# Conditioning products on four 32-column parts, plain, and layer 0's shift and scale made in quarters of the columns

## The chip, the cores and the metric

One core of one Trainium2 chip runs the whole program. The metric is the device time of one execution in microseconds (us), the median of several runs. TensorE (PE, with its weight loads as PEld), VectorE (DVE), ScalarE (ACT), GpSimd (POOL) and SyncE (SP, which here issues the transfers of weights) each work through a queue of their own in order.

## What is computed

The reference runs two transformer blocks over 256 tokens of width 1024. The change lies in the first block, which has two layers and also carries 256 context tokens. Each layer first makes a modulation of 3072 columns from a conditioning vector, once for the latent tokens and once for the context tokens:

```python
def layer(x, cx, c_silu, cctx_silu, norm_w, ada_w, ada_b, w_in, w_out, ...):
    mod = c_silu @ ada_w + ada_b
    mod_c = cctx_silu @ ada_w + ada_b
    shift, scale, gate = jnp.split(mod, 3, axis=-1)
    hx = rmsnorm(x, norm_w) * (1 + scale[:, None, :]) + shift[:, None, :]
    hc = rmsnorm(cx, norm_w) * (1 + scale_c) + shift_c
    px = split_cols(hx @ w_in)          # queries, keys, values of three mixers, and a gate of 1536
    ...                                  # three kinds of attention
    ux = jnp.concatenate([ya, yb, yc_], axis=-1) * jax.nn.silu(px[9])
    x = x + gate[:, None, :] * (ux @ w_out)
```

So the product with `ada_w` (1024 x 3072, two layers, 25 MB in all) has only two rows, and `hx`, from which everything else follows, can't be made before shift and scale of its columns are there. The rest (the second block: feed-forward, two sparse attentions, feed-forward, twice) isn't touched.

## The kernel before

All weights come in tiles of 128 partitions x 1024 elements (512 KB), in the order of `weight_plan`. SP loads tile after tile into staging buffers `ws` (18 of their own for the start, then four in turn, `LOOK`), ACT copies a tile into a rounded high part `wh` (L283) and DVE makes the low part `wl` (L284), three buffers of each, and PE multiplies a matrix product as three rounded products: high x high, high x low, low x high (`three`, L423 to L425). As soon as DVE has split a tile, its staging buffer is free for the next transfer.

A conditioning tile holds two chunks of 128 rows by 512 columns, and there are 48 of them. The first 16 (layer 0's shift and scale, in two halves of the columns) are multiplied as they are, in full precision, out of the staging buffers (L748): the conditioning is a 32-column weight operand `cst1`, and the tile's two chunks go to columns 0 to 31 and 32 to 63 of the array, so to two 32-row strips of one accumulator `psm`. A plain product stands as two records in the trace. The other 32 (layer 1's, and layer 0's gate) are split like all weights and multiplied in rounded form, four products to a tile, against an 8-column operand `cst4` that holds the high and low parts of the conditioning (L751, L753). These are the fills: they are spread over the products that make gate columns 4 to 11 of layer 0, four tiles within each (`gate` in `layer1`), eight tiles to an accumulator.

When an accumulator is done, `ada_close` copies it (ACT, L764), adds its rows up and turns them with four small products (L767), and DVE adds the bias and forms 1 + scale (L778, L783).

`start` orders the beginning: `norm_rows` makes the normalised rows `xn` and `cn`, then for each half of the columns `cond` multiplies eight tiles and closes, `half` turns the rows on PE (`turn_pair`, L812), applies scale and shift on ACT (`ht`, L821) and splits the result on DVE into `hT` (L824, L825); `gate` multiplies the first four gate columns with what is there of `hT`. All later products need the whole of `hT`. A scheduler places the instructions on each engine's queue, by priorities in the order written and by what is ready; PE does them in that order.

Attention runs between the weight products. Its last step multiplies probabilities and values on two 64-column parts of the array (L609), 4 to 20 products to an accumulator.

## Time and profile before

| | us |
|---|---|
| median of 3 runs | 1919.62 (1919.45 to 1920.26) |
| the profiled execution's own time | 1919.23 |
| its span, first to last instruction | 1917.4 |
| PE busy in it | 1876.4 |
| DVE busy | 1263.4 |
| ACT busy | 1094.2 |

The span is the profiled execution without what lies around it, 1.8 us. PE's busy time is that of pipelined products whose ends are modelled: two products that follow each other closely overlap in it, so what one costs is read from start to start and not from its duration.

### The profile page before, as it was taken

How to read it: one execution, taken by the hardware profiler on the slowest of the kernel's cores; microseconds unless marked ns; L12 is line 12 of the kernel's file. 1: busy time of each engine (PE TensorE's matmuls, PEld its weight loads, DVE VectorE, ACT ScalarE, POOL GpSimd, SP SyncE). 2: the span in 40 equal slices, each digit the busy share in tenths (PEclk: the TensorE clock that was granted, in tenths of full speed). 3: DMA queues.
4: the chain of work that ended last, by engine and by line, in shares of the span. 5: the costliest groups of instructions: out<-in, count | busy, mean ns of one | idle time of the engine just before them, and what ended most of it. 6: DMA issues, size and time to landing. Idle time of an engine off the chain costs nothing.

```text
span 1917.4 us, 27602 instructions
## 1 busy us (share of the span) xinstructions
PE 1876.4 (98%) x10332; PEld 1549.6 (81%) x10332; DVE 1263.4 (66%) x2476; ACT 1094.2 (57%) x1971; POOL 4.9 (0%) x14
## 2 busy tenths in 40 slices
PE   7999999999999999999999999999999999999998
PEld 3777788877988977888888878888888888888886
DVE  3476856788586787555688565555555689575555
ACT  3467757785567675444477655445444558655443
POOL 0000000000000000000000000000000000000000
PEclk9999999999999999999999999999999999999999
DMA  7334344136432238554434665554555333555551
GB/s 310 109 121 133 120 99 133 67 122 210 134 98 86 69 110 291 188 182 148 123 104 130 229 209 187 188 186 176 191 186 183 115 102 115 199 184 178 187 185 68
DMA packets 85670, 295.16 MB, mean 154 GB/s; under 512 B 10144, under 2 KB 10656, under 8 KB 85536
## 3 DMA queue, kind: packets, MB, share of 16 engines
q1 hardware_dynamic: 80304, 282.34, 45.2%
q10 hardware_dynamic: 5136, 11.04, 1.8%
q8 instruction: 81, 1.33, 0.3%
q14 instruction: 53, 0.43, 0.1%
q0 software_dynamic: 96, 0.01, 0.1%
HBM read 292.30 MB, written 1.06 MB: 153 GB/s over the span
## 4 chain that ended last, share of the span: by engine, by line
PE 90%; DVE 6%; ACT 2%; DMA 1%; issue 1%; SPq 0%; ACTq 0%; DVEq 0%
PE acc L423 24%; PE acc L425 24%; PE acc L424 23%; PE pso L609 4%; PE pst L577 4%; PE pss L511 2%; PE pss L512 2%; DVE wl L284 2%; PE psr L714 1%; PE psx L1195 1%; PE psr L720 1%; PE psm L1277 1%; DMA ws<-in_wall 1%; PE acc L751 1%; PE acc L753 1%
## 5 line engine op out<-in xcount | busy, mean ns | idle before, releaser
L284 DVE TENSOR_TENSOR wl<-ws,wh 128x1024 fp32r<-128x1024 f32 (+3 forms) x530 | 628.0, 1187 | 455.9 <-ACT wh L283 454.7
L283 ACT CAST wh<-ws 128x1024 fp32r<-128x1024 f32 (+3 forms) x530 | 541.4, 1024 | 531.3 <-PE acc L425 476.9
L423 PE MATMUL acc<-wh,xt 128*128 128x512 f32 (+3 forms) x1120 | 416.2, 375 | 1.6 <-ACT wh L283 1.6
L424 PE MATMUL acc<-wl,xt 128*128 128x512 f32 (+3 forms) x1120 | 415.2, 371 | 1.4 <-DVE wl L284 1.4
L425 PE MATMUL acc<-wh,xt 128*128 128x512 f32 (+3 forms) x1120 | 414.8, 372 | 0.0
L424 PEld LDWEIGHTS acc<-wl,xt 128*128 128x128 f32 x1120 | 211.0, 188 | 34.1 <-DVE wl L284 2.9
L423 PEld LDWEIGHTS acc<-wh,xt 128*128 128x128 f32 x1120 | 210.5, 188 | 34.1 <-ACT wh L283 2.3
L425 PEld LDWEIGHTS acc<-wh,xt 128*128 128x128 f32 x1120 | 210.6, 188 | 32.7 <-issue 0.7
L423 PE MATMUL acc<-wh,hT 128*128 128x384 f32 (+2 forms) x480 | 159.5, 333 | 0.0
L424 PE MATMUL acc<-wl,hT 128*128 128x384 f32 (+2 forms) x480 | 158.6, 330 | 0.0
L425 PE MATMUL acc<-wh,hT 128*128 128x384 f32 (+2 forms) x480 | 157.9, 329 | 0.0
L547 ACT ACTIVATE p<-pss,nm 128x512 f32<-128x512 f32 (+2 forms) x240 | 127.7, 541 | 27.7 <-DVE nm L530 12.0
L423 PE MATMUL acc<-wh,hffn 128*128 128x512 f32 x352 | 137.8, 391 | 0.0
L425 PE MATMUL acc<-wh,hffn 128*128 128x512 f32 x352 | 137.1, 390 | 0.0
L424 PE MATMUL acc<-wl,hffn 128*128 128x512 f32 x352 | 137.0, 389 | 0.0
L577 PE MATMUL pst<-consts,p 128*128 128x128 f32 x624 | 101.4, 277 | 0.8 <-ACT pt L593 0.7
L423 PEld LDWEIGHTS acc<-wh,hT 128*128 128x128 f32 x480 | 90.6, 189 | 6.4 <-issue 0.4
L424 PEld LDWEIGHTS acc<-wl,hT 128*128 128x128 f32 x480 | 90.7, 189 | 5.5 <-issue 0.4
L425 PEld LDWEIGHTS acc<-wh,hT 128*128 128x128 f32 x480 | 90.6, 189 | 4.5 <-issue 0.4
L577 PEld LDWEIGHTS pst<-consts,p 128*128 128x128 f32 x624 | 73.0, 140 | 24.1 <-ACT pt L593 4.9
L569 ACT ACTIVATE p<-p,rinv 128x256 f32<-128x256 f32 (+2 forms) x152 | 81.3, 577 | 11.6 <-DVE rinv L563 8.5
L425 PEld LDWEIGHTS acc<-wh,hffn 128*128 128x128 f32 x352 | 66.1, 188 | 13.9
(302 smaller groups left out, 2825.8 us busy)
## 6 DMA issues: line engine op xcount, KB each, us to landing
ws<-in_wall SPq DMA_DIRECT2D x476, 512.0 KB, 3.4
ws<-in_wall SPq DMA_DIRECT2D x64, 384.0 KB, 3.2
bias<-in_bias ACTq DMA_DIRECT2D x8, 512.0 KB, 3.9
cx<-in_ctx SPq DMA_DIRECT2D x2, 1024.0 KB, 6.7
ws<-in_wall SPq DMA_DIRECT2D x4, 420.0 KB, 3.1
gt<-gates ACTq DMA_DIRECT2D x3, 512.0 KB, 4.6
x<-in_x SPq DMA_DIRECT2D x1, 1024.0 KB, 6.8
out<-y SPq DMA_DIRECT2D x2, 512.0 KB, 2.6
```

The costliest lines, as they stand in the source:

```text
L283: self.nc.scalar.copy(h[:, :n], s[:, :n])
L284: self.nc.vector.tensor_tensor(lo[:, :n], s[:, :n], h[:, :n].bitcast(F32), op=ALU.subtract)
L423: mm(out, ah, bh, start=start, stop=False)
L424: mm(out, ah, bl, start=False, stop=False)
L425: mm(out, al, bh, start=False, stop=stop)
L511: nc.tensor.matmul(S[:, o:o + w], q, kh, start=True, stop=False)
L512: nc.tensor.matmul(S[:, o:o + w], q, kl, start=False, stop=True)
L547: nc.scalar.activation(p[:, o:o + w], S[:, o:o + w], AF.Exp, bias=nm[:, i:i + 1], accum_out=sm[:, i:i + 1])
L569: nc.scalar.activation(p[:, o:o + w], p[:, o:o + w], AF.Copy, scale=r[:, i:i + 1])
L577: nc.tensor.transpose(t[:, i * P:(i + 1) * P], sl["P"][:, o:o + P], self.ident)
L609: nc.tensor.matmul(O[HD * i:HD * i + HD, c:c + w], v, p, start=y < 2, stop=y >= len(todo) - 2)
L714: nc.tensor.transpose(p[:, 2 * a + g, :], ks[:, t, a, g, :], self.ident_r)
```

## The change

It does five things. First, every conditioning tile is now used plain, out of its staging buffer, and two tiles are taken together: `ada_pair` multiplies their four chunks on four 32-column parts of the array (columns 0, 32, 64 and 96) into the four strips of one accumulator, the later tile's chunks first. The rounded form, `cst4` and its preparation are gone. Second, layer 0's shift and scale are made in four quarters: a quarter has 256 columns of scale and 256 of shift, four tiles, and is followed in the plan by one tile of two row chunks of `w_in` for gate columns 0 to 3 (`quarter_tiles`); after a quarter is closed, two column chunks of `hT` follow, and 24 gate products on them. Third, a fill takes its two pairs after row chunks 1 and 6 of a gate column; the plan puts the second pair behind the first tile of the next item, and `w_hold` fetches that tile ahead. Fourth, a staging buffer that holds a plain tile becomes free only when its products are done: `_pump` stops at such a tile, and is called again behind each pair. Fifth, `in_a_row` writes each group of products on parts (the four of a pair, and attention's of one accumulator) so that the scheduler puts nothing between them.

```diff
-START_TILES = 18
-START_PLAIN = [*range(8), *range(9, 17)]
+START_TILES = 5 * QUARTERS
...
+def quarter_tiles(i):
+    w = r_(1024 + 256 * i, 256) + r_(256 * i, 256)
+    return split_tiles("ada_w", 0, KD, w) + [("w_in", 0, r_(2 * i, 2), r_(3072, P * GATE_START))]
...
+            plan += t[:1] + late + t[1:]
+            n = it[2] if gate else 0
+            plan += fill[:n // 2]
+            late, fill = fill[n // 2:n], fill[n:]
...
-        if self.si in START_PLAIN:
+        if name == "ada_w":
             self.split[self.si] = (s, s)
+            self.plain.add(self.si)
...
+    def _pump(self):
         while self.di < min(max(self.si, START_TILES) + self.LOOK + self.more * (self.di < self.more_end), len(self.plan)):
+            if self.di - self.LOOK >= START_TILES and self.di - self.LOOK in self.plain:
+                break
             self._dma()
...
+    def in_a_row(self, todo):
+        def mm(out, a, b, start, stop):
+            return self.nc.tensor.matmul(out, a, b, start=start, stop=stop)
+        first = mm(*todo[0])
+        with self.tc.issue_after(getattr(first, "ins", first)), self.tc.high_priority():
+            for x in todo[1:]:
+                mm(*x)
...
+    def ada_pair(self, g):
+        b = g["n"] // 2
+        todo = []
+        for j in range(2):
+            ks, _, w, _ = self.w_next("ada_w", *g["blocks"][b])
+            todo += [(kk, w[:, i, :]) for i, kk in enumerate(ks)]
+        self.in_a_row([(g["bank"][32 * i:32 * i + 32, :], self.cst1[:, kk, 28 - 4 * b:60 - 4 * b], w,
+                        g["n"] == 0, g["n"] == g["last"]) for i, (kk, w) in enumerate(todo[::-1])])
+        self.plain -= {self.wi - 2, self.wi - 1}
+        self._pump()
         g["n"] += 1
...
+        quarter(0)
+        self.gate_acc = [self.acc() for _ in range(GATE_START)]
+        for i in range(QUARTERS):
+            ks, _, wh, wl = self.w_next("w_in", 0, 3072)
             for a, kk in enumerate(ks):
+                for j in range(GATE_START):
+                    self.three(self.gate_acc[j], ...
+                if a == 0 and i + 1 < QUARTERS:
+                    quarter(i + 1)
...
-                    if k * n // KD < (k + 1) * n // KD:
+                    if n and k in (1, 6):
+                        if k == 6:
+                            self.w_hold()
                         self.fill = self.fill or self.ada_open(self.fills.pop(0), "a")
-                        self.ada_tile(self.fill)
+                        self.ada_pair(self.fill)
```

Three places show what moves. On PE at the very start, the queue before has the first half's eight tiles (`ws`, two products each), its close (`psr`) and the first turned rows (`psx`):

```order
L748 MATMUL psm_221<-ws_121,cst_100 32x512 x2
L748 MATMUL psm_221<-ws_123,cst_100 32x512 x2
L748 MATMUL psm_221<-ws_125,cst_100 32x512 x2
L748 MATMUL psm_221<-ws_127,cst_100 32x512 x2
L748 MATMUL psm_221<-ws_129,cst_100 32x512 x2
L748 MATMUL psm_221<-ws_131,cst_100 32x512 x2
L748 MATMUL psm_221<-ws_133,cst_100 32x512 x2
L748 MATMUL psm_221<-ws_135,cst_100 32x512 x2
L767 MATMUL psr_252<-consts,mod_250 128x4 x4
L812 MATMUL psx_263<-consts,xn_0_159 128x128 x4
L812 MATMUL psx_273<-consts,xn_1_160 128x128 x4
```

and now:

```order
L446 MATMUL psm_215<-ws_113,cst_94 32x512 x2
L446 MATMUL psm_215<-ws_111,cst_94 32x512 x2
L446 MATMUL psm_215<-ws_117,cst_94 32x512 x2
L446 MATMUL psm_215<-ws_115,cst_94 32x512 x2
L792 MATMUL psr_238<-consts,mod_236 128x2 x4
L859 MATMUL psx_246<-consts,xn_0_153 128x128 x4
L859 MATMUL psx_256<-consts,xn_1_154 128x128 x4
L455 MATMUL acc_266<-hT_0_100,wh_228 128x512
```

The close and the first turned rows stand behind four tiles instead of eight, and gate products follow them at once. On PE in the first gate column with fills (gate column 4; `wh`, `wl` and `hT` make the gate product, `cst` the fill), before:

```order
L423 MATMUL acc_687<-hT_0_110,wh_615 128x512
L424 MATMUL acc_687<-hT_1_111,wh_615 128x512
L425 MATMUL acc_687<-hT_0_110,wl_616 128x512
L751 MATMUL acc_694<-wh_645,cst_96 8x512
L753 MATMUL acc_694<-wl_646,cst_96 8x512
L751 MATMUL acc_694<-wh_645,cst_96 8x512
L753 MATMUL acc_694<-wl_646,cst_96 8x512
L423 MATMUL acc_687<-hT_0_110,wh_615 128x512
```

and now the second pair of the same gate column:

```order
L457 MATMUL acc_680<-hT_0_100,wl_621 128x512
L446 MATMUL acc_687<-ws_696,cst_94 32x512 x2
L446 MATMUL acc_687<-ws_624,cst_94 32x512 x2
L455 MATMUL acc_680<-hT_0_100,wh_620 128x512
L456 MATMUL acc_680<-hT_1_101,wh_620 128x512
```

Four rounded products to a tile become four plain ones to two tiles, and they read `ws` itself. Fifteen gate products lie between the first pair and this one. On SP the transfers of the tiles around it, with what each waits for, before:

```order
L257 DMA ws_559<-in_wall 128x1024 [waits DMAHW7_49,DMAHW3_49,DVE_49]
L257 DMA ws_589<-in_wall 128x1024 [waits DMAHW0_49,DVE_49]
L257 DMA ws_619<-in_wall 128x1024 [waits DMAHW5_49,DMAHW1_49,DVE_49]
L257 DMA ws_649<-in_wall 128x1024 [waits DMAHW6_49,DMAHW2_49,DVE_49]
L257 DMA ws_685<-in_wall 128x1024 [waits DMAHW3_49,DVE_49]
```

and now:

```order
L264 DMA ws_624<-in_wall 128x1024 [waits DMAHW7_49,DMAHW5_49,DVE_49]
L264 DMA ws_696<-in_wall 128x1024 [waits DMAHW4_49,DVE_49]
L264 DMA ws_698<-in_wall 128x1024 [waits DMAHW3_49,PE_49]
L264 DMA ws_700<-in_wall 128x1024 [waits DMAHW2_49,DMAHW0_49,PE_49]
L264 DMA ws_824<-in_wall 128x768 [waits DMAHW6_49,DMAHW1_49,PE_49]
L264 DMA ws_826<-in_wall 128x1024 [waits DMAHW5_49,PE_49]
```

Where every transfer waited for DVE's split of an earlier tile, those that follow a plain tile in its buffer now wait for PE. From layer 0's output product on, the queues of all engines stand as before.

## Rows read from the trace of the kernel before

**Rows 1.** The page: span, busy time and instructions by engine, and the chain that ended last.

```profile
span 1917.4 us, 27602 instructions
PE 1876.4 (98%) x10332; PEld 1549.6 (81%) x10332; DVE 1263.4 (66%) x2476; ACT 1094.2 (57%) x1971; POOL 4.9 (0%) x14
...
PE 90%; DVE 6%; ACT 2%; DMA 1%; issue 1%; SPq 0%; ACTq 0%; DVEq 0%
```

**Rows 2.** Groups of PE instructions, 65 to 340 us: busy us, mean ns, idle before.

```profile
L425 PE MATMUL acc<-hT,wl 128*128 128x512 f32 x65 | 26.1, 402 | 1.2 <-DVE wl L284 1.2
...
L753 PE MATMUL acc<-wl,cst 128*8 128x512 f32 x64 | 25.4, 398 | 0.1
L751 PE MATMUL acc<-wh,cst 128*8 128x512 f32 x64 | 25.4, 397 | 0.0
```

**Rows 3.** Timeline of PE, one fill tile: start us, us, engine, line, operation.

```profile
88.17 0.40 PE L751 MATMUL acc<-wh,cst 128*8 128x512 f32 x1
...
89.09 0.40 PE L423 MATMUL acc<-hT,wh 128*128 128x512 f32 x1
```

**Rows 4.** Timeline of TensorE in the start, its weight loads (PEld) at one place.

```profile
12.10 7.37 PE L748 MATMUL psm<-ws,cst 128*32 128x512 f32 x24 [12.10 <-DMA ws<-in_wall]
...
19.70 0.14 PEld L748 LDWEIGHTS psm<-ws,cst 128*32 128x32 f32 x4 [1.14 <-DMA ws<-in_wall]
19.70 1.05 PE L748 MATMUL psm<-ws,cst 128*32 128x512 f32 x4 [0.23 <-DMA ws<-in_wall]
...
20.97 1.05 PE L748 MATMUL psm<-ws,cst 128*32 128x512 f32 x4 [0.22 <-DMA ws<-in_wall]
22.76 1.05 PE L767 MATMUL psr<-consts,mod 64*128 64x4 f32 x8 [0.73 <-ACT mod L764]
23.74 0.65 PE L812 MATMUL psx<-consts,xn 128*128 128x128 f32 x4
...
36.75 0.39 PE L425 MATMUL acc<-hT,wl 128*128 128x512 f32 x1
37.07 6.20 PE L748 MATMUL psm<-ws,cst 128*32 128x512 f32 x26
43.19 0.50 PE L423 MATMUL acc<-hT,wh 128*128 128x512 f32 x1
...
54.03 1.20 PE L423 MATMUL acc<-hT,wh 128*128 128x512 f32 x4 [0.17 <-DVE hT L824]
...
65.05 0.39 PE L423 MATMUL acc<-wh,hT 128*128 128x512 f32 x1
```

**Rows 5.** Timeline of PE: plain products on one 32-column part, 128 columns each.

```profile
948.92 6.27 PE L1277 MATMUL psm<-w,mv 128*32 128x128 f32 x56 [0.23 <-issue]
```

**Rows 6.** Timelines of ACT and DVE in the start.

```profile
24.48 1.02 ACT L821 ACTIVATE ht<-psx,mod 128x256 f32<-128x256 f32 x2 [1.78 <-DVE mod L778]
...
51.22 1.92 ACT L821 ACTIVATE ht<-psx,mod 128x256 f32<-128x256 f32 x4
...
17.02 1.41 DVE L804 TENSOR_SCALAR xn<-cx,rstd 128x1024 f32<-128x1024 f32 x2
```

**Rows 7.** Busy time by stretch: us, engines (instructions), PEclk granted, DMA share, GB/s.

```profile
26.00:28.00 2.00, 2.00 (x4) 0.18 (x2) 2.00 (x3) 2.00 (x5) 0.00 (x0) 0.50 1.04 414
28.00:30.00 2.00, 2.00 (x7) 0.90 (x6) 1.88 (x4) 1.00 (x3) 0.00 (x0) 0.65 1.02 406
...
100.00:120.00 20.00, 19.51 (x113) 14.89 (x112) 17.75 (x38) 9.58 (x14) 0.00 (x0) 1.00 0.59 201
```

**Rows 8.** The page: splitting of weight tiles, and transfers (KB, us to landing).

```profile
L284 DVE TENSOR_TENSOR wl<-ws,wh 128x1024 fp32r<-128x1024 f32 (+3 forms) x530 | 628.0, 1187 | 455.9 <-ACT wh L283 454.7
L283 ACT CAST wh<-ws 128x1024 fp32r<-128x1024 f32 (+3 forms) x530 | 541.4, 1024 | 531.3 <-PE acc L425 476.9
...
ws<-in_wall SPq DMA_DIRECT2D x476, 512.0 KB, 3.4
```

**Rows 9.** Timeline of PE: attention's products on two parts, broken once.

```profile
226.80 0.65 PE L609 MATMUL pso<-pt,VG 128*64 128x256 f32 x4
227.39 0.55 PE L577 MATMUL pst<-consts,p 128*128 128x128 f32 x3
227.86 3.24 PE L609 MATMUL pso<-pt,VG 128*64 128x256 f32 x28
```

More of the change, by code (lines that the diff above doesn't have):

```diff
@@ L69 @@
 ]
-def gate_half_tiles(h):
-    return [("w_in", 0, r_(4 * h, 4), r_(3072 + 256 * i, 256)) for i in range(GATE_HALF // 2)]
+def quarter_tiles(i):
+    w = r_(1024 + 256 * i, 256) + r_(256 * i, 256)
+    return split_tiles("ada_w", 0, KD, w) + [("w_in", 0, r_(2 * i, 2), r_(3072, P * GATE_START))]
 WOUT_KS = [[0, 1], [4, 2], [3, 5], [8, 9], [6, 10], [11, 7]]
@@ L107, in weight_plan @@
     plan = []
-    a = [[t for l, c0 in g for t in ada_tiles(l, [c0])] for g in ADA_HALF + [sum(ADA_FILL, [])]]
-    g = [gate_half_tiles(h) for h in range(2)]
-    plan += a[0] + g[0][:1] + a[1] + g[0][1:] + g[1]
-    fill = a[2]
+    for i in range(QUARTERS):
+        plan += quarter_tiles(i)
+    fill = [t for l, c0 in sum(ADA_FILL, []) for t in ada_tiles(l, [c0])]
     for l in range(DEPTH):
+        late = []
         for it in ITEMS[l]:
-            if it[0] == "g":
-                plan += split_tiles("w_in", l, KD, r_(3072 + 128 * it[1], 128)) + fill[:it[2]]
-                fill = fill[it[2]:]
-            else:
-                plan += split_tiles("w_in", l, KD, bundle_cols(*it))
+            gate = it[0] == "g"
+            t = split_tiles("w_in", l, KD, r_(3072 + P * it[1], P) if gate else bundle_cols(*it))
+            plan += t[:1] + late + t[1:]
+            n = it[2] if gate else 0
+            plan += fill[:n // 2]
+            late, fill = fill[n // 2:n], fill[n:]
         for stream in range(2 if l == 0 else 1):
@@ L171, in const_table @@
     put("ident", np.eye(P))
+    e = np.arange(P)[:, None] % 32
+    put("sel2", (2 * (e // 4) + e % 4 == np.arange(16)[None, :]) & (e % 4 < 2))
     nf = HD // 4
@@ L194, in const_table @@
     put("hsel", (np.arange(64)[:, None] // 16 == np.arange(4)[None, :]).astype(np.float32))
[L195 to L196 removed]
     return [np.concatenate(x, 1).astype(np.float32) for x in parts], where
+FIRST = P + 16
 COLS = {}
@@ L235, in __init__ @@
         self.ratio = 1.0
+        self.plain = set()
+        self.held = None
         self.flags = set()
@@ L607, in f_v @@
                 todo += [(i, c + pair[2], P, v, p) for i, c, v, p in pair[1].get("extra", [])]
-            for y, (i, c, w, v, p) in enumerate(todo):
-                nc.tensor.matmul(O[HD * i:HD * i + HD, c:c + w], v, p, start=y < 2, stop=y >= len(todo) - 2)
+            self.in_a_row([(O[HD * i:HD * i + HD, c:c + w], v, p, y < 2, y >= len(todo) - 2)
+                           for y, (i, c, w, v, p) in enumerate(todo)])
             for pair in pairs:
@@ L735, in ada_open @@
     def ada_open(self, blocks, kind):
[L736 to L755 removed]
+        return dict(blocks=blocks, bank=self.acc() if kind == "a" else self.ps(kind), n=0, last=len(blocks) * 2 - 1)
@@ new lines, in ada_cols @@
+    def ada_cols(self, g):
+        nb = len(g["blocks"])
+        self.uid += 1
+        m = self.junk.tile([P, 512], F32, tag="junk", name=f"mod{self.uid}")
+        self.nc.scalar.copy(m, g["bank"])
+        p = self.ps("r")
+        for j in range(4):
+            self.nc.tensor.matmul(p[:, 16 * j:16 * j + 2 * nb], m[:, j * P:(j + 1) * P], self.cst("sel2")[:, :2 * nb],
+                                  start=True, stop=True)
+        return p[:, :64].rearrange("p (j b s) -> p s b j", b=8, s=2)
@@ new lines, in ada_quarter @@
+    def ada_quarter(self, i):
+        nc = self.nc
+        g = self.ada_open([(0, 1024 + 256 * i)], "m")
+        for _ in range(2):
+            self.ada_pair(g)
+        pv = self.ada_cols(g)[:, :, 0, :]
+        for a, j in ((8, 0), (0, 2)):
+            o = a + 2 * i
+            nc.vector.tensor_tensor(self.mod[0][:, :, o:o + 2], pv[:, :, j:j + 2],
+                                    self.col("ada_b", o, 2)[:, None, :].to_broadcast([P, 2, 2]), op=ALU.add)
+        o = 8 + 2 * i
+        nc.vector.scalar_tensor_tensor(self.mod[0][:, :, o:o + 2], self.mod[0][:, :, o:o + 2], 1.0,
+                                       self.col("norm_w", 2 * i, 2)[:, None, :].to_broadcast([P, 2, 2]),
+                                       op0=ALU.add, op1=ALU.mult)
@@ L760, in ada_close @@
         nb = len(g["blocks"])
-        self.uid += 1
-        m = self.junk.tile([P, 512], F32, tag="junk", name=f"mod{self.uid}")
-        rows = g.get("rows", 4 * nb)
-        nc.scalar.copy(m[:rows, :], g["bank"][:rows, :])
-        p = self.ps("r")
-        for j in range(4):
-            nc.tensor.matmul(p[:, 16 * j:16 * j + 2 * nb], m[:rows, j * P:(j + 1) * P],
-                             self.cst("sel2")[:rows, :2 * nb], start=True, stop=True)
-        pv = p[:, :64].rearrange("p (j b s) -> p s b j", b=8, s=2)
+        pv = self.ada_cols(g)
         b = 0
```

79 lines of the change are left out of this document (22 added, 57 removed).

## The prediction

> **What bounds the kernel now.** I read the page first: PE is busy 98% of the span and carries 90% of the chain that ended last [rows 1], so I looked for places where PE itself does less, or waits less. The groups by line between 65 and 340 us came next [rows 2]: the rounded fills are 128 products there, and PE hardly waits for their parts; the one visible wait in that stretch is 1.2 us for DVE's `wl`. A timeline of one fill tile gives its price [rows 3]: from its first product at 88.17 to the next gate product at 89.09 is 0.92 us, four products at 0.23 us, in a stream without a hole. So a fill tile removed from PE's queue there is 0.92 us off the end, as long as nothing else becomes the bound. The start is different: its timeline [rows 4] shows PE waiting for weights until 12.10, for single tiles until 20.97, and then working nearly without a stop until the first product that needs the whole of `hT`, at 65.05. That moment is the start's measure.
>
> **Part by part. Fills on four parts.** Before: 32 tiles x 0.92 = 29.4 us on PE. Now: 16 groups of four plain products. The rows show two parts at work, never four. On one part, 56 records of 128 columns take 6.27 us, 0.112 us each, so 0.448 us for 512 columns and 0.90 us for a product of two records [rows 5]. On two parts, 26 records take the 6.12 us from 37.07 to 43.19, 0.235 us each [rows 4]: twice the rate, the parts run side by side, and two products, one on each part, pass in 0.94 us. An isolated set of one product on each of two parts also shows 1.05 us, with the tail of its last result in it. If four parts run side by side as two do, a group takes the same 0.94 us. Going to parts costs 0.09 us (36.75 to 37.07 is 0.32 where 0.23 is usual) and coming back 0.11 (the product at 43.19 lasts 0.50 where 0.39 is usual) [rows 4]. That makes 1.14, say 1.15 us, for what cost 1.84: 16 x 0.69 = **11.0 us gained**. The ends: 1.05 us a group (12.6 us gained) and, if only two parts ever run together, two rounds, 2.08 us (3.8 us lost). I take the first, since from one part to two the rate doubled without a loss, and since the two parts' loads and streams begin together: at 19.70 four weight loads occupy 0.14 us beside products that start at 19.70 as well [rows 4].
>
> One rule speaks against that. The Trainium skill, TensorE: Matmul & The Clock Gate, Part 3 (The mechanism), says that a weight load overlaps running products only where the row groups differ, and column parts share theirs. By it a group's eight loads would come on top of its products; at four in 0.14 us that is 0.28 us a group, 4.5 us in 16, and the fills would give 6.5 us. This case's trace disagrees, by the loads at 19.70 just named, and the result would lie inside the forecast's own range. The same part gives 2.38 times for three column parts: by that figure, as an estimate, four would run at 0.79 of full concurrency, a group would cost 1.4 us, and the fills would give 7 us instead of 11. No row here shows more than two.
>
> The splits of these tiles go with the products: 32 x 1.02 us of ACT and 32 x 1.19 us of DVE [rows 8], 71 us in all. Neither bounds the stage as a whole, though DVE is at 17.75 of 20 us in its fullest stretch [rows 7]. I count a part of the 1.2 us wait for `wl` [rows 2]: **0.5 us gained**, between 0 and 1.2. The larger worth of it is that ACT and DVE don't become the bound when PE gets faster.
>
> **Staging.** A plain tile holds its staging buffer until PE is through, and there are four. The transfer takes 3.4 us to land [rows 8]. Three kinds of place follow from the order. Where a pair's second transfer waits for the pair before it, in the same gate column, only 15 gate products may lie between: 15 x 0.23 = 3.45 us, against 3.4 plus the issue. That is so at two of the four doubles of gate columns; at the others 12 transposes or more lie between. Where the second pair of a double's first gate column waits for the split of the held tile, the chain is 1.02 + 1.19 + 3.4 = 5.6 us from the start of that gate column, against 6 x 0.23 + 1.15 + 3.45 = 6.0 us on PE: covered by 0.4 us, and not where ACT or DVE has other work queued ahead, at 89% of DVE's time [rows 7]. This is so four times. Queued behind a late transfer is every later tile on SP, and on PE the gate column's last chunk and attention. I price two places at 0.5 us and three at 0.5: **2.5 us lost**, between 0 and 8 (four doubles at 2 us, a DVE queue of one or two larger operations).
>
> **The start in quarters.** Tiles arrive every 1.27 us (12.10 to 19.70 is six of them) [rows 4]. The first quarter's four are there at 12.10 + 3 x 1.27 = 15.9 instead of eight at 20.97. Its last pair may run at half the clock, as TensorE does between 26 and 28 us after a stretch with little work [rows 7], 2 us instead of 1.05: 17.9. From the last pair's start to the close's products the row shows 1.8 us, 1.05 of it the pair (20.97 to 22.76), then 0.98 to the turned rows (23.74), 1.7 from the close to the first `ht` (22.76 to 24.48) [rows 4, 6]: so the close at 17.9 + 0.8 = 18.7 and `ht` at 20.4. From `ht` for two streams to the first gate product there was 2.8 us (51.22 to 54.03) [rows 4, 6]: 23.2. `cn`, ready at 18.4 (17.02 + 1.41) [rows 6], is no later than the close. I take 23 us, between 21.5 and 24. Behind that PE has: 96 gate products x 0.23 = 22.1; six pairs x 1.15 = 6.9; three closes x 0.98 = 2.9; six sets of four turned rows at some 0.6 (0.65 with the tail [rows 4]) = 3.6; together 35.5 us. To it come one stretch at the low clock as before, half of 2 us and 0.35 of 2 us [rows 7], 1.7 us; 0.8 us in the last quarter, where only three gate products stand between the last turned rows and the products that need them; and some 1.5 us of short waits. 23 + 35.5 + 4.0 = 62.5 against 65.05: **2.5 us gained**, between 0.5 (a second stretch at the low clock) and 6.5 (gate products from 21.5, and half the waits). The last tiles land at about 37 us, before PE comes to them, so transfers don't bound it. More than the tiles that come earlier, the six groups at 1.15 instead of two parts' 0.94 for each two products help.
>
> **Runs kept whole.** Of attention's 32 accumulators 28 already stand in one piece; four are broken, five breaks in all. One break costs about 0.15 to 0.3 us: 227.39 to 227.86 is 0.47 for three transposes [rows 9]. **0.7 us gained**, between 0 and 1.5, or a little lost where a held run must wait for its last operand.
>
> The queues from layer 0's output product on stand as before, and I put nothing there.
>
> **Sum.** 11.0 + 0.5 - 2.5 + 2.5 + 0.7 = 12.2 us. Against the profiled execution's 1919.2 that is 1907.0; its time is 0.4 us below the median of the runs, so **1907.4 us** for the median.
>
> **The rivals.** *Late tiles eat it.* Staging costs 8 us and the start gives 0.5: 11.0 - 8 + 0.5 + 0.5 + 0.5 = 4.5 us, **1915 us**. For it: four buffers, a cover of 0.4 us, a full DVE. Against: the attention work between, and that DVE has 38 us less to do. *The change doesn't free PE.* Attention's chain over ACT and DVE sets the pace of the stage once PE is lighter, and fills gone from PE show up as waits: only the start's 2.5 us stays, about **1917 us**, within 0.2%. Against: 1.2 us of visible wait in 275 us [rows 2]. *Four parts run two at a time*, because the array is fed with no more than two streams: a group costs 2.08 us. Fills lose 3.8; the six pairs in the start lose 6 x 0.94 = 5.6 more, so the start loses 3.1; staging is better covered and costs 1; runs give 0.7. The sum is 7 us lost: **1927 us, slower**. It decides from 1.84 us a group. Nothing in the rows excludes it but the clean doubling from one part to two.
>
> **How the numbers follow.** Chances: the forecast 0.66, late tiles 0.17, PE not freed 0.08, two at a time 0.09. The forecast's own range, with groups of 1.05 to 1.4 us and the other terms' bounds not all at one end, is 1899 to 1912. To leave out no more than 2 in 10 the range must take in the late tiles: **1898 to 1917**. A measurement of this kernel can tell about 0.2%, 3.8 us, from no change, so faster begins below 1915.8. The forecast lies there, and of the late tiles 0.13: faster 0.79, same 0.12 (the rest of the late tiles and PE not freed), slower 0.09.
>
> **What would show it.** Right: in the profile after, the four products of a pair as eight records that start in two sets of four, the second some 0.45 us behind the first, and 1.1 to 1.2 us from the group's start to the next gate product; no L751 or L753; the first product with the whole of `hT` at about 62 us; splits fewer by 32 on ACT and on DVE. Late tiles would show as idle time of PE ahead of the pairs, put down to transfers of `ws`, half a microsecond at a time. Two at a time would show as records starting in sets of two, or groups of 2 us. PE not freed would show as waits for ACT or DVE in attention's transposes between 100 and 430 us. The forecast is wrong if the stage from 65 us to the end of layer 0's attention doesn't shorten by 5 us or more, or if the time after about 450 us changes at all.

## The result

The changed kernel takes **1902.47 us** (median; 1901.73 to 1903.15) against 1919.53 us (1919.29 to 1920.26): a ratio of 0.9912 with a 95% interval of 0.9899 to 0.9926, so 17.1 us (14 to 19 us by the interval) are gained. The prediction was 1907.4 us, 12.2 us gained, with a range of 1898 to 1917. The profiled execution of after has a span of 1899.9 us, 17.5 us shorter than that of before.

The page of after answers [rows 1] and [rows 8]: span, busy time by engine, the chain that ended last, and the splits of weight tiles (line, busy us, mean ns, idle before).

```profile
span 1899.9 us, 27515 instructions
...
PE 1858.9 (98%) x10348; PEld 1542.5 (81%) x10348; DVE 1228.5 (65%) x2439; ACT 1064.7 (56%) x1941; POOL 4.9 (0%) x14
...
PE 93%; DVE 4%; DMA 2%; ACT 1%; issue 1%; ACTq 0%; DVEq 0%
...
L292 DVE TENSOR_TENSOR wl<-ws,wh 128x1024 fp32r<-128x1024 f32 (+2 forms) x498 | 589.4, 1185 | 441.2 <-ACT wh L291 440.0
L291 ACT CAST wh<-ws 128x1024 fp32r<-128x1024 f32 (+2 forms) x498 | 508.0, 1023 | 508.0 <-PE acc L457 481.5
```

PE's busy time falls by 17.5 us, exactly as the span does, and PE is still 98% busy and still the bound. The 32 splits on each of ACT and DVE are gone (530 to 498).

Where the time went is read from five moments on PE's timeline, the same in both kernels. "Start" ends with the first product that needs the whole of `hT`; "gates" ends with the last gate product of layer 0 and holds all 16 fills; then the rest of attention and the output products up to the first on `uc`; then up to the first product on `xt`; then to the last product. Us, worked out from the starts of these products in each trace; the other columns are experiments that follow.

| stretch | before | after | two parts | old start | quarters, two parts | warm | warm, gaps too | gate first |
|---|---|---|---|---|---|---|---|---|
| start | 65.05 | 62.32 | 61.02 | 64.60 | 63.50 | 59.52 | 58.40 | 58.12 |
| gates | 252.89 | 238.38 | 252.90 | 238.54 | 238.59 | 238.63 | 238.77 | 238.71 |
| to the first `uc` | 122.05 | 123.10 | 122.10 | 123.33 | 123.43 | 122.85 | 123.25 | 120.89 |
| `uc` to `xt` | 299.91 | 298.49 | 301.43 | 298.50 | 299.25 | 298.47 | 298.14 | 300.89 |
| the rest | 1168.03 | 1168.09 | 1168.17 | 1168.11 | 1167.99 | 1168.03 | 1168.08 | 1168.05 |

From before to after that is -2.73, -14.51, +1.05, -1.42 and +0.06 us. Nearly all lies where the prediction put it, in the start and the fills, and nothing behind 720 us.

The fill of after, timelines of PE and of its weight loads (start us, us, engine, line, operation); it answers [rows 3]:

```profile
85.22 0.39 PE L457 MATMUL acc<-hT,wl 128*128 128x512 f32 x1
85.53 1.07 PE L446 MATMUL acc<-ws,cst 128*32 128x512 f32 x8
86.53 0.50 PE L455 MATMUL acc<-hT,wh 128*128 128x512 f32 x1
86.86 0.39 PE L456 MATMUL acc<-hT,wh 128*128 128x512 f32 x1
```

```profile
85.53 0.16 PEld L446 LDWEIGHTS acc<-ws,cst 128*32 128x32 f32 x8 [0.35 <-ACT VG L687]
```

A group of four products is 1.00 us from its first record to the next gate product. Going in adds 0.08 us (85.22 to 85.53 is 0.31 where 0.23 is usual), coming out 0.10 (86.53 to 86.86): 1.18 us. The eight weight loads take 0.16 us in all and lie beside the running products. In the records four products start within 25 ns of each other and the second four 0.45 us later.

The last group of the fills is the one place where a transfer comes late:

```profile
298.68 0.39 PE L457 MATMUL acc<-hT,wl 128*128 128x512 f32 x1
299.13 1.06 PE L446 MATMUL acc<-ws,cst 128*32 128x512 f32 x8
```

From start to start that is 0.45 us where 0.31 is usual; in the trace TensorE is idle for 0.07 us of it, until the group's last tile lands.

The waits of PE that are long enough to be listed, between 17 and 420 us in after (what was waited for: us in total, times, longest):

```profile
PE acc L455 <- DVE hT L871: 2.8, 2, 1.8
PE psr L792 <- ACT mod L789: 0.8, 1, 0.8
PE pst L609 <- ACT pt L625: 0.8, 1, 0.8
```

No wait of a fill for a transfer is among them, and the 1.2 us wait for `wl` of [rows 2] is gone. The start of after answers [rows 4]:

```profile
13.20 1.94 PE L446 MATMUL psm<-ws,cst 128*32 128x512 f32 x8 [13.20 <-DMA ws<-in_wall]
15.67 1.94 PE L446 MATMUL psm<-ws,cst 128*32 128x512 f32 x8 [0.53 <-DMA ws<-in_wall]
18.36 1.87 PE L792 MATMUL psr<-consts,mod 128*128 128x2 f32 x8 [0.76 <-ACT mod L789]
...
23.87 2.07 PE L455 MATMUL acc<-hT,wh 128*128 128x512 f32 x4 [1.83 <-DVE hT L871]
25.74 0.63 PE L456 MATMUL acc<-hT,wh 128*128 128x512 f32 x1
...
28.73 0.63 PE L457 MATMUL acc<-hT,wl 128*128 128x512 f32 x1
29.28 1.07 PE L446 MATMUL psm<-ws,cst 128*32 128x512 f32 x8
...
62.32 0.39 PE L455 MATMUL acc<-wh,hT 128*128 128x512 f32 x1
```

Here a group lasts 1.94 us and a gate product 0.63, against 1.07 and 0.39 from 29.28 on: TensorE has stood idle until 13.20, and runs at half rate, 1.2 of its 1.2 and 2.4 GHz, through the waits of the chain and then from 23.87 to 29 without a hole. The column of the granted clock reads 1.00 in these microseconds, because the trace's first entry of that clock begins only at 29.30. That it is the clock is read from the length of the records: products of 0.63 us also stand at 425.76 and, in the run with seven unused products, from 23.4 to 26 us, both below, where the column does fall. In [rows 7]'s low stretch a lone plain product takes 1.84 us from start to start instead of 0.98.

Before starts at half rate as well, which the merged first line of [rows 4] hides. The plain products up to 15.6 us (ns, shortest, median and longest):

```profile
L748 PE MATMUL psm<-ws,cst x10: 717/1060/1062, 12.1 to 15.5; 128*32 128x512 f32 x10
```

The tiles at hand keep TensorE at work there without a hole up to 19.5 us, and its records are down to 592 to 617 ns from 16.05 on; the four tiles of a quarter leave the holes of 0.53, 0.76 and 1.83 us shown above, and the low rate lasts to 29.3.

### The profile page after: what moved, and what is told of

It is laid out like the page before. It is cut to its first block, busy times and chain, and to the rows that moved or that the text cites. A ratio compares the mean times of both kernels' runs of the same rounds, so it can differ in the third digit from the quotient of the medians.

```text
span 1899.9 us, 27515 instructions
## 1 busy us (share of the span) xinstructions
PE 1858.9 (98%) x10348; PEld 1542.5 (81%) x10348; DVE 1228.5 (65%) x2439; ACT 1064.7 (56%) x1941; POOL 4.9 (0%) x14
## 4 chain that ended last, share of the span: by engine, by line
PE 93%; DVE 4%; DMA 2%; ACT 1%; issue 1%; ACTq 0%; DVEq 0%
PE acc L455 25%; PE acc L457 25%; PE acc L456 24%; PE pso L446 4%; PE pst L609 4%; PE pss L543 2%; PE pss L544 2%; PE psr L746 1%; PE psx L1231 1%; DVE wl L292 1%; PE psr L752 1%; PE acc L446 1%; PE psm L1313 1%; DMA ws<-in_wall 1%; ACT wh L291 1%; DMA gt<-gates 1%
## 5 line engine op out<-in xcount | busy, mean ns | idle before, releaser
L292 DVE TENSOR_TENSOR wl<-ws,wh 128x1024 fp32r<-128x1024 f32 (+2 forms) x498 | 589.4, 1185 | 441.2 <-ACT wh L291 440.0
L291 ACT CAST wh<-ws 128x1024 fp32r<-128x1024 f32 (+2 forms) x498 | 508.0, 1023 | 508.0 <-PE acc L457 481.5
L457 PEld LDWEIGHTS acc<-wh,hffn 128*128 128x128 f32 x352 | 66.1, 188 | 13.9
```

The lines of the kernel that those rows point to most:

```text
L291: self.nc.scalar.copy(h[:, :n], s[:, :n])
L292: self.nc.vector.tensor_tensor(lo[:, :n], s[:, :n], h[:, :n].bitcast(F32), op=ALU.subtract)
L457: mm(out, al, bh, start=False, stop=stop)
```

## The experiments

All stand on the changed kernel unless said, and each ratio is to the kernel before, measured beside it. That kernel's median was 1919.05 to 1919.55 us in these series, so a difference of two medians, such as those from after below, is uncertain by about half a microsecond on that account alone.

**Fills on two parts.** The theory is that the fills' gain is four parts working side by side; the rival, that it came from the splits and staging that go away with the rounded form.

```diff
-        self.in_a_row([(g["bank"][32 * i:32 * i + 32, :], ...
+        self.in_a_row([(g["bank"][32 * (i % 2):32 * (i % 2) + 32, :], ...
```

> The changed kernel, with the 16 groups of fills on two 32-column parts instead of four (two products on each part, still held together); the start keeps four parts. Theory A, the gain in the fills is PE time that four parts side by side save: a group becomes four records a part, 4 x 0.43 = 1.72 us plus some 0.3 for going to parts and back, 2.0 instead of 1.16 us, so 16 x 0.85 = 13 to 14 us come back and the median is about 1916 us. Rival B, the gain comes from the 32 splits that ACT and DVE no longer make, and PE's products there were partly hidden: at most 4 us come back, 1903 to 1906 us.

Measured: 1917.8 us, ratio 0.9995 (0.9986 to 1.0005), 15.3 us more than after. PE's timeline:

```profile
84.23 1.91 PE L446 MATMUL acc<-ws,cst 128*32 128x512 f32 x8
86.07 0.50 PE L455 MATMUL acc<-hT,wh 128*128 128x512 f32 x1
```

A group costs 1.84 us from start to start instead of 1.00, and the gates take 252.90 us, those of before to 0.01 us. The splits are gone in this kernel too, and with two parts that bought nothing: the whole gain of the fills is the third and fourth part.

**The splits done all the same.** The fills' tiles are also split, as before, into a scratch tile that nothing reads; ACT and DVE get their 71 us back.

```diff
+            if self.si >= START_TILES:
+                h = self.wp.tile([P, WT], mybir.dt.bfloat16, tag="xh", ...)
+                self.nc.scalar.copy(h[:, :n], s[:, :n])
+                self.nc.vector.tensor_tensor(h[:, :n], s[:, :n], h[:, :n], op=ALU.subtract)
```

> The changed kernel, but ACT and DVE still make a copy and a subtraction of each of the 32 fill tiles, into a scratch tile that nobody reads (71 us of work in all put back); the plain products stay. Theory A: PE is the bound, and only waits of PE for ACT and DVE come back, 0 to 2 us: 1902.5 to 1904.5 us. Rival B: the relief of ACT and DVE is the gain: 5 us or more come back, 1907.5 us and above. A third, that the scratch holds the staging buffer longer and makes tiles late, would show as waits of PE for transfers of ws ahead of the groups.

Measured: 1903.03 us, 0.9913 (0.9898 to 0.9928). The gates take 238.42 us against 238.38. No wait for a transfer of `ws` shows either. ACT and DVE had the room.

**The products of a group not held together.**

```diff
-        self.in_a_row([(...) for i, (kk, w) in enumerate(todo[::-1])])
+        for i, (kk, w) in enumerate(todo[::-1]):
+            self.nc.tensor.matmul(..., start=g["n"] == 0, stop=g["n"] == g["last"])
```

> The eight products of a conditioning group are no longer kept in one run: the planner may put other products between them, and does so in about half of the groups (pieces of 4, of 3 and 1, of 7 and 1). All else as in the changed kernel. Theory A, the gain needs the four parts side by side: each product that stands alone costs two more changes of parts and 0.4 to 0.9 us in place of its quarter of a step, for some 15 broken groups 4 to 9 us, so 1906.5 to 1911.5 us. Rival B, the planner breaks them only where TensorE would have waited anyway, or pieces of four cost nothing: 1901.5 to 1903.5 us.

Measured: 1910.39 us, 0.9961 (0.9947 to 0.9974), 7.9 us more than after. One of the broken groups:

```profile
95.69 1.04 PE L779 MATMUL acc<-ws,cst 128*32 128x512 f32 x2
96.66 0.53 PE L752 MATMUL psr<-ident_r,qs 128*128 128x128 f32 x4
97.03 0.50 PE L746 MATMUL psr<-ident_r,ks 128*128 128x128 f32 x4
97.46 1.06 PE L779 MATMUL acc<-ws,cst 128*32 128x512 f32 x6
```

One product alone (two records) takes about as long as four together, 0.98 us from start to start against 1.00. In the trace five of the 16 groups are broken, each into one product and three. The gates grow by 5.8 us, of which 4.8 are the groups themselves; the start, whose groups are free here as well, ends at 63.95. Five broken groups cost the gates two fifths of the 14.5 us that the four parts give.

**Three staging buffers instead of four.** This was to settle the prediction's staging term.

```diff
-    LOOK = 4
+    LOOK = 3
```

> Three staging buffers for weight tiles in place of four, all else as in the changed kernel. The prediction charged the fills 2.5 us (0 to 8) because a group now holds two staging buffers until it ends; the trace of the changed kernel shows no wait of TensorE for a staged tile behind 17 us. Theory A, the tiles come well ahead, since the transfer of one takes 3.4 us and a group comes only about every 8 us: even three buffers give no wait of more than 1 us in the fills, and the time is 1902 to 1904 us. Rival B, four buffers were just enough: TensorE waits for ws ahead of most groups, 0.2 to 0.5 us each and 5 to 12 us in all, and the time is 1907 to 1915 us.

Measured: 1913.52 us, 0.9973 (0.9962 to 0.9983). The total is the rival's, the place is not. In the gates PE waits 2.0 us for transfers, at two of the 16 groups, and the stretch is 1.7 us longer than in after (240.11):

```profile
150.98 1.07 PE L446 MATMUL acc<-ws,cst 128*32 128x512 f32 x8 [0.91 <-DMA ws<-in_wall]
```

The profiled execution is 2.1 us above the median here, and the rest of its span's 13.9 us lies elsewhere: 5.1 up to `uc`, 2.6 up to `xt`, 5.5 behind it, less 1.2 in the start (PE's waits for `wh` grow from 2.1 to 5.9 us; the rest is not followed up here). With four buffers the fills are at the edge in two places only: in the trace of after the last tile of the eighth and of the 16th group lands 0.14 and 0.04 us ahead of it, that of every other group 0.9 to 31 us. Other places need the fourth buffer more.

**The old start.** Halves of eight tiles on two parts, as before, with everything else as after.

```diff
-QUARTERS = 4
-START_TILES = 5 * QUARTERS
+ADA_HALF = [[(0, 1024), (0, 0)], [(0, 1536), (0, 512)]]
+START_TILES = 18
```

> The changed kernel with the start of the kernel before: halves of the columns, two parts, eight tiles a half; fills and attention as in the changed kernel. Theory A: the start's gain, 62.32 against 65.05 us for the first product with the whole of hT, is kept to the end: 2.7 us come back, 1904.2 to 1906.2 us. Rival C: the start's 2.7 us is used up later, by waits that don't depend on it: 1902.5 us. Rival D: much of the gain of 17 us hangs on the quarters, over the order of tiles and the gate columns behind them: 1908 us and above.

Measured: 1905.06 us, 0.9923 (0.9909 to 0.9938): 2.6 us more than after, 2.3 in the start, kept to the end.

**Quarters, but their groups on two parts.** The prediction held that the six groups on four parts do more for the start than the tiles that come earlier.

```diff
-        return dict(..., last=len(blocks) * 2 - 1)
+        return dict(..., last=len(blocks) * 2 - 1, parts=4 if kind == "a" else 2)
```

> The changed kernel, with the start's eight groups on two parts instead of four; quarters and fills as changed. Theory A: behind the first quarter the start is PE's work, so the six later groups cost 0.85 us more each, 5 us, and the first two, at half the clock, add up to 1.7 us each less what the arrival of tiles hides: 1907 to 1910 us, that is, quarters without four parts are worse than the halves of before. Rival E: the start hangs on the arrival of tiles and on the chain from a quarter's close to its gate products, and PE's part hides: 0 to 2 us, 1902.5 to 1904.5 us.

Measured: 1903.34 us, 0.9913 (0.9898 to 0.9928), and `hT` at 63.50: 1.2 us later, where 5 were expected. A miss.

```profile
13.11 5.67 PE L446 MATMUL psm<-ws,cst 128*32 128x512 f32 x16 [13.11 <-DMA ws<-in_wall]
19.50 1.05 PE L796 MATMUL psr<-consts,mod 64*128 64x2 f32 x8 [0.72 <-ACT mod L793]
...
21.52 1.91 PE L446 MATMUL psm<-ws,cst 128*32 128x512 f32 x8
23.82 0.50 PE L455 MATMUL acc<-hT,wh 128*128 128x512 f32 x1 [0.39 <-DVE hT L875]
...
24.89 0.40 PE L457 MATMUL acc<-hT,wl 128*128 128x512 f32 x1
```

The groups of the start cost 6.8 us more by start to start, but two groups of two parts keep TensorE at work from 13.1 to 18.8 with hardly a hole, and from 17.3 on it runs at full rate: the close takes 1.05 us instead of 1.87, a gate product 0.40 instead of 0.63. The slower form of the groups buys back the clock that the faster form loses. The order differs too: the second quarter's first group stands at 21.52, in the wait for `hT`, and the first gate product begins at 23.82 even so (23.87 in after).

**TensorE kept warm.** If the low clock is what the start loses, work without use ahead of the first tile must give it back, in which case the result beats both kernels.

```diff
+        warm = self.ps("o")
+        for _ in range(7):
+            nc.tensor.matmul(warm[:60, :480], self.cst1[:, 0, :], self.cst1.rearrange("p k n -> p (k n)"), ...)
```

> Seven products whose result nobody reads (60 rows of output, 480 columns, fp32) are put on TensorE ahead of the first weight tile, to fill the time in which it would stand idle; all else is the changed kernel. In the changed kernel the records show TensorE at half rate from its first product at 13.2 us to 29.3 us (a record of the first groups 1062 ns, of the gate products 628 ns, against 617 and 389 ns later). Theory A, the low clock at the start is a standing cost of the start and lasts because nothing keeps TensorE busy ahead of it: the first groups and the small products after them run at full rate, whole hT comes 2 to 5 us earlier than 62.3 us, and the time is 1897.5 to 1900.5 us. Rival B, the waits in the chain (second tile at 15.7 us, mod, hT) let the clock fall again: records of 1062 or 628 ns come back behind 18 us, and the time is 1901.5 to 1902.5 us. Rival C, the first block is ended by something else than TensorE: no change.

Measured: **1899.50 us**, 0.9899 (0.9886 to 0.9913), 3.0 us less than after.

```profile
5.36 7.82 PE L912 MATMUL pso<-cst 128*60 128x480 f32 x14 [5.36 <-DVE cst L1619]
13.35 1.06 PE L446 MATMUL psm<-ws,cst 128*32 128x512 f32 x8 [0.16 <-DMA ws<-in_wall]
15.90 1.06 PE L446 MATMUL psm<-ws,cst 128*32 128x512 f32 x8 [1.50 <-DMA ws<-in_wall]
17.73 1.05 PE L792 MATMUL psr<-consts,mod 128*128 128x2 f32 x8 [0.76 <-ACT mod L789]
18.64 1.18 PE L859 MATMUL psx<-consts,xn 128*128 128x128 f32 x8
21.96 1.20 PE L455 MATMUL acc<-hT,wh 128*128 128x512 f32 x4 [2.14 <-DVE hT L871]
...
23.39 0.63 PE L457 MATMUL acc<-hT,wl 128*128 128x512 f32 x1
...
26.50 1.06 PE L446 MATMUL psm<-ws,cst 128*32 128x512 f32 x8
```

```profile
24.00:26.00 2.00, 2.00 (x7) 1.47 (x5) 0.00 (x0) 0.00 (x0) 0.00 (x0) 0.50 1.02 406
```

Both A and B happen: the first groups and the turned rows run at full rate, and after the waits of 1.50, 0.76 and 2.14 us the gate products still fall to half rate, from 23.0 to 26.4. The second fence is a row of stretches as in [rows 7]: the granted clock, behind the five engines, is 0.50.

**The gaps filled as well**: unused products behind the two groups of the first quarter and behind its turned rows.

```diff
+                self.warm_up(w[:, :60], 1 + 2 * a, 240)
...
+                warm_up(self.mod[0][:, 0, 0:2], 5, 240)
```

> As the run with seven unused products ahead of the first tile, and unused products (240 columns) also in the gaps of the chain: one behind the first group, three behind the second, five while hT is made. Theory A, the clock stays up if the gaps are filled: gate products at 389 ns from their first on, whole hT 4 to 6 us earlier than 62.3 us, time 1896.5 to 1898.5 us. Rival B, the unused products get into the way of the chain (each is 0.4 us at full rate) as much as they save: no more than 1 us better than with the seven alone. Rival C, the clock is low there whatever TensorE does: records at half rate to about 29 us and the time within 1 us of 1902.5.

Measured: **1898.85 us**, 0.9894 (0.9881 to 0.9908).

```profile
16.92 1.43 PE L917 MATMUL pso<-cst,ws 128*60 128x240 f32 x6
18.27 1.05 PE L793 MATMUL psr<-consts,mod 128*128 128x2 f32 x8
...
22.51 1.20 PE L455 MATMUL acc<-hT,wh 128*128 128x512 f32 x4
23.54 0.39 PE L456 MATMUL acc<-hT,wh 128*128 128x512 f32 x1
```

No product of the start behind 13 us is at half rate any more; `hT` is whole at 58.40, 3.9 us earlier than in after, and the time falls by 3.6. The gaps add 1.1 us in the start to what the first seven products give, less than the 1.6 us of half rate that they remove (eight products, 0.43 us from start to start instead of 0.23), since everything from the close on comes 0.55 us later: the close stands directly behind the three unused products of the second group, at 18.27 against 17.73, and the first gate product begins at 22.51 against 21.96.

**Attention's runs not held together.**

```diff
-            self.in_a_row([(O[...], v, p, y < 2, y >= len(todo) - 2) for y, (i, c, w, v, p) in enumerate(todo)])
+            for y, (i, c, w, v, p) in enumerate(todo):
+                nc.tensor.matmul(O[...], v, p, start=y < 2, stop=y >= len(todo) - 2)
```

> The attention's products of probabilities by values are not kept in one run any more: of 32 runs the planner breaks three (two in two, one in three pieces); all else as in the changed kernel. Theory A, as the prediction has it, each broken piece costs two more changes between whole and parts (0.1 us each) and the pause that they bring: 0.7 us, so 1903.2 us (1902.7 to 1904). Rival B, the planner breaks them where TensorE would have waited, so nothing or a small gain: 1902 to 1902.6 us.

Measured: 1903.66 us, 0.9917 (0.9904 to 0.9931): 1.2 us more, with intervals that overlap. In the trace the broken products take 0.61 us more by start to start, four breaks at 0.15 us. Another difference is larger, and it isn't shown to come from the breaks: the wait ahead of `uc` is longer.

```profile
425.18 0.80 PE L455 MATMUL acc<-wh,uc 128*128 128x512 f32 x1 [4.16 <-DVE tmp L1168]
```

**The end of layer 0's block.** In after the gain at this place shrinks for a while: 17.2 us at the last gate product, 15.5 at the last attention product (432.5 to 417.0). PE's timeline and the granted clock (PEclk, the figure after the five engines):

```profile
421.06 0.39 PE L457 MATMUL acc<-wh,u 128*128 128x512 f32 x1
423.80 0.50 PE L455 MATMUL acc<-wh,uc 128*128 128x512 f32 x1 [2.35 <-DVE tmp L1168]
...
425.76 0.63 PE L456 MATMUL acc<-wl,uc 128*128 128x512 f32 x1
...
428.94 0.40 PE L455 MATMUL acc<-wh,uc 128*128 128x512 f32 x1
```

```profile
424.00:429.00 5.00, 5.00 (x16) 3.92 (x16) 5.00 (x9) 2.20 (x5) 0.00 (x0) 0.66 0.79 255
```

In before some 40 products on `u` stood behind the last attention product, ten of them even behind the first on `uc`, and there was no wait; now there are 17, and the others ahead of it, so PE is through before DVE's `tmp` frees an accumulator, and then runs at half rate for 3.4 us. In the same stretch DVE is busy for 5.00 of 5 us, the third figure of the row. The first try to remove this loaded half of the gate vector ahead of attention's last stage and put `tmp` ahead of ten splits of `uc`. In it the reload of `ctx` stood ahead of splits that read the old contents, so `uc` is made from other data, and these splits wait for that transfer (ACT 4.36 us).

> At the end of the first block, on the changed kernel: the first half of the gate vector is loaded ahead of the last attention stage into a buffer of its own, and ten of the twelve splits of uc stand on VectorE behind the two products tmp that free the first accumulators, instead of ahead of them. Theory A, of the 17 us that are gained up to the last gate product some 4 us go at this place, to a wait of 2.4 us of TensorE for the accumulators (tmp came 0.5 us late behind the load of the gate vector and 4 us late behind the splits) and to the 1.7 us that the half rate from 425 to 429 us then costs: the wait falls under 0.5 us, no record of the uc products is at half rate, and the time is 1898.5 to 1900.5 us. Rival B, the chain from the last attention product to uc sets the place (split of u, wl of the next tile): the wait stands under another name, and the time is 1901.5 to 1903 us. Rival C, the planner lays the end of the block otherwise and gives the gain back in it: no change.

Measured: 1909.06 us, 0.9936 (0.9923 to 0.9950): 6.6 us more than after, worse than any of the three said; C comes nearest. The planner laid the stretch from 312 us on otherwise, and the wait for `tmp` of 0.75 us was followed by one for weights, held up on ACT behind the late splits:

```profile
433.33 0.50 PE L455 MATMUL acc<-wh,uc 128*128 128x512 f32 x1 [2.32 <-ACT wh L291]
```

The same edit together with the filled gaps:

> The unused products in the start's gaps and the early gate vector at the end of the first block together. Theory A, the two costs lie at different places and add up: 3.6 us and what the early gate vector brings alone, so 1895 to 1897 us if that is 2 to 4 us. Rival B, they are the same slack counted twice: no better than the better one alone, 1898 to 1899 us.

1904.67 us, 0.9923 (0.9909 to 0.9936): neither theory's time, since the edit itself costs time; it says nothing on whether the two add up. The second try leaves PE's order alone and reloads `ctx` last; it stands on the kernel with the filled gaps.

```diff
+                    gate0 = wp.tile([P, 512], F32, name=f"gt0{l}")
+                    nc.scalar.dma_start(gate0, self.gates[l][0:1, 0:4]...)
...
-                    for c in [c for ks in WOUT_KS for c in ks]:
+                    uc_split([c for ks in WOUT_KS[:2] for c in ks])
...
+                    if need:
+                        uc_split([] if ct == 0 else [c for ks in WOUT_KS[2:] for c in ks])
```

> On the kernel with unused products in all the start's gaps, and with the order of the first block's end alone changed: the half of the gate vector that the first two tmp need is loaded first, in a transfer of 256 KB, and only four of the twelve splits of uc stand ahead of tmp on VectorE; the reload of ctx follows the last split. TensorE's order up to the first uc product is as without this edit. That kernel waits 2.6 us for an accumulator at 420.4 us and then runs products at half rate. Theory A, this wait and the half rate are a cost of their own: tmp starts some 2 us earlier, the wait falls under 0.8 us, no uc product is at half rate, and the time is 1895.5 to 1897.5 us against 1898.85. Rival B, VectorE's work at this place (splits, tmp, x and the next weights' wl) sets the time: what is saved ahead of uc comes back as waits for wl behind it, and the time is 1898 to 1900 us.

Measured: **1898.00 us**, 0.9888 (0.9872 to 0.9905).

```profile
417.49 0.39 PE L457 MATMUL acc<-wh,u 128*128 128x512 f32 x1
417.72 0.39 PE L455 MATMUL acc<-wh,uc 128*128 128x512 f32 x1
...
421.79 0.50 PE L456 MATMUL acc<-wl,uc 128*128 128x512 f32 x1 [0.64 <-DVE wl L292]
...
427.50 0.50 PE L456 MATMUL acc<-wl,uc 128*128 128x512 f32 x1 [1.05 <-DVE wl L292]
```

The wait and the half rate are gone, `uc` begins 2.7 us earlier, and yet `xt` begins at the same time (718.6 in both): the time comes back, 2.2 us of it by the end of the products on `uc`, where 2.3 us of waits for `wl` and `wh` stand, and the last half microsecond by `xt`. The time is rival B's, and the waits for `wl` fit its reason, that DVE's work at this place sets its end and the wait for `tmp` was one form of it; a run with less work on DVE there, which would show it, was not made. This is the fastest of the kernels, 0.9 us ahead of the one that it stands on, which the intervals do not tell from no difference.

## Why the prediction was right, and where not

**Fills: right in the mechanism, a little low.** A group was put at 1.15 us and costs 1.18. Four parts do run side by side: two rounds of 0.45 us, and the two-part kernel gives back all of the gates' 14.5 us. The rule that was weighed, from the Trainium skill (TensorE: Matmul & The Clock Gate, Part 3, The mechanism: a weight load overlaps running products only where the row groups differ), does not agree with this trace: eight loads pass in 0.16 us beside the products, and a group of four with eight loads takes 1.00 us where a product alone with two takes 0.98. The same part's 2.38 times for three column parts gave 1.4 us a group as an estimate, which is not what came either; three parts were not run. What was too low is the side of before. 0.92 us a tile is one undisturbed tile; over all 32 the products of the fills take 31.9 us from start to start, the wait for `wl` among it, 2.4 us more than 32 x 0.92. The prediction counted 0.5 us of that. With 16 groups of 1.18, 18.9 us, the fills give 13.0 us where 11.0 and 0.5 were put; of the 1.5 us that are left of the gates' 14.5, 0.9 are waits for `ks` and `qs` in before that are gone in after, and two breaks of attention's runs are some 0.3.

**Relief of ACT and DVE: half a microsecond that it isn't.** With the splits kept the gates are as short. The wait for `wl` is gone there too, so it did not go because DVE has less to do; what removed it, the plain groups or the other order, is not told apart.

**Staging: the term that was wrong.** It was priced at 2.5 us lost (0 to 8), and cost 0.07 us (up to 0.3 in the other kernels with four buffers). The working named the places well and their cover badly. Where only 15 gate products lie between two pairs, at two of the four doubles, the last tile does land at the last moment, 0.14 and 0.04 us ahead of its group; but that costs next to nothing. At the four places where a cover of 0.4 us was worked out, the second group of each double, the tiles land 5.8 to 13.7 us ahead in the trace of after. The chain over the split of the held tile was taken to start with the gate column; those transfers are issued 2.9 us or more ahead of it. With three buffers two groups wait, for 2.0 us. This term, and the 1.5 us by which the fills gave more than 11.5, are 4.0 of the 4.9 us between 12.2 and the 17.1 measured.

**Start: the right sum for a wrong reason.** 62.5 us was forecast, 62.32 came, and the old start costs 2.6 us in the end. That is partly luck. The low clock was put at one pair and 1.7 us of gate products; it ran from the first product to 29.3 us, over both pairs, the close, the turned rows and 12 gate products, which lost 2.7 us by it (5.44 us from start to start, 0.23 each otherwise). The first gate product came 0.9 us later than the 23 forecast, the low clock took 1.0 us more behind it, and the groups and gate products with the changes between them 0.8 more; against that the closes and turned rows took 5.0 us where 6.5 was put, and the waits 0.94 where 2.3 was put. These cancel. That the six groups on four parts help more than the tiles that come earlier isn't shown: from the old start to quarters on two parts `hT` comes 1.1 us earlier, from there to four parts 1.2.

Nor are these differences sharper than a microsecond and a half. In six kernels with the same start (after, the fills on two parts, the splits kept, three buffers, attention's runs free, the first try at the block's end) TensorE reaches the full rate that lasts through the fills between 26.6 and 29.4 us, and `hT` is whole between 60.8 and 62.3; after lies at the late end. In three of the six the granted clock is up for a while from 17.2 to 17.8 us on and falls again at 20.6 to 21.2. Against the early end the old start loses 3.8 us instead of 2.3, and the seven unused products give 1.2 instead of 2.8.

**Runs kept whole: about right.** 0.7 us forecast; 0.61 us by the trace, 1.2 us by times that don't tell it from nothing.

**Behind 450 us: a little, where nothing was put.** The last 1168 us are the same to 0.1 us. But the queues don't stand as before from layer 0's output product on; PE's is the same from 459 us of before (441 of after), in the middle of the products on `uc`. Ahead of that a wait of 1.26 us for DVE's `xn` at 455 us of before is gone in after; behind it after gives back 0.6 us up to `xt`. By its own sign, that the time behind 450 us must not change at all, the prediction was wrong in this small part.

**The rivals.** Late tiles came at one group, with 0.07 us, and two at a time did not come, as the group's length shows. "The change doesn't free PE" came true in one place only, the end of layer 0's block, where PE waits 2.35 us for DVE; there is no net loss around `uc`, +1.05 and -1.42 us.

## What to carry to other kernels

Small products of 32 output rows belong on four column parts, written so that nothing comes between them: one alone costs as much as four. When a faster form leaves TensorE with holes at the start of a kernel, look at the length of the first records, not at the clock column alone; a few unused products ahead of the first tile gave 3 us here, about as much as the whole rebuilding of the start (2.6). A wait that a trace names is worth its length only if the engine behind it isn't full: here 2.5 us of wait were removed, and waits of 2.3 us came in their place.

## What the runs showed of the hardware

Two column parts take 1.84 us for four plain products of 512 columns, four parts 1.00: nearly twice the rate again, with eight weight loads in 0.16 us beside the products. Changing from whole-array products to parts costs 0.08 us, changing back 0.10.

TensorE, idle until its first product at 13.20 us, ran at half rate for 16 us of work with holes. Where it had work without a hole from its first product on it came to full rate at 15.8 us (before, first product at 12.10) and 17.3 us (quarters on two parts, first product at 13.11). Where unused products stood ahead of the first tile, their own records shrink from 1007 to 566 ns at 9.4 us and the first tile runs at full rate; with only these seven the products behind a wait of 2.14 us were at half rate again. The same start came to full rate at times up to 2.8 us apart in six kernels.
